# Softmax over rows of 1024: ACT's code aligned to slot 100 of a block of 128 instructions, and 25 buffers in place of 4 for the small tiles

## The chip, the core and the metric

The kernel runs on one core of a Trainium2 chip. A core has engines that run their own instruction streams and wait for one another through semaphores. Four of them matter here: VectorE (DVE in the profile), ScalarE (ACT), GpSimd (POOL) and SyncE (SP). Data moves between the memory of the device (HBM) and the core's own memory (SBUF) by DMA; a transfer is issued from the queue of an engine (here SP, POOL and ACT) and carried out in packets by 16 DMA engines that all queues share.

The metric is the device time of one execution in microseconds (us). Lower is better. Beside the plain runs there is one profiled execution, from which all views of the profile come.

## The reference

```python
def setup_inputs():
    batch, seq, dim = 32, 512, 1024
    return {
        "x": np.random.randn(batch, seq, dim).astype(np.float32),
        "temperature": 0.5,
    }

def reference(x: np.ndarray, temperature: float) -> np.ndarray:
    scaled = x / temperature
    shifted = scaled - np.max(scaled, axis=-1, keepdims=True)
    exp_x = np.exp(shifted)
    return (exp_x / np.sum(exp_x, axis=-1, keepdims=True)).astype(np.float32)
```

That is a softmax over the last axis of 16,384 rows of 1024 float32 numbers: 67.11 MB are read and 67.11 MB are written.

## The kernel before

The 16,384 rows are cut into 11 passes (`PASSES`, line 10). A pass takes 128 partitions times k rows for each partition: 11 rows in the first pass, 12 in each of the nine that follow, 9 in the last. The tile of a pass is one buffer of the pool `data`, which has 4 (line 43); so pass i + 4 can be loaded only when pass i has been stored. A pass is worked on in groups, of 4, 4 and 3 rows in the first, of 6 and 6 in the next nine, and of 4, 3 and 2 in the last. There are 24 groups.

Each group goes through four steps:

- `maximum` (lines 65 to 74): DVE takes the maximum of each row (line 71, into the small tile `top`) and multiplies it by the negative scale (line 74, into `bias`). Each group takes four new small tiles here, `top`, `bias`, `sums` and `recip`, from the pool `stats`, which has 4 buffers for each name (line 44).
- `exponential` (lines 76 to 87): ACT computes the exponential of each row in place and leaves the row's sum in `sums`. Each row is one call on line 80, and two instructions on ACT: ACTIVATE, and ACTIVATION_READ_ACCUMULATOR, which writes the sum. All groups together have 128 such pairs.
- `divide` (lines 89 to 100): DVE takes the reciprocal of the sums (line 92) and multiplies the rows by it: in one instruction for the whole group in passes 2, 3, 4 and 6 (line 95), row by row in the others (line 98).
- `store` (lines 102 to 111): after the last group of a pass the whole tile is stored by one DMA, from POOL's queue in passes 0 to 5 and from ACT's queue in passes 6 to 10 (line 110). Then `load` issues the next load from SP's queue (line 62). Ahead of the first store, POOL copies one element of tile 2 (line 108), so that this store waits until tile 2 has landed.

The order of the work on each engine is the order of the program (`manual_schedule`, line 115). In the steady part, DVE does the maximum of group g + 1 between the maximum and the division of group g, while ACT works on a group's exponentials. From pass 9 on a pass begins only when the groups before it are finished (`ALONE`); the three groups of the last pass have all their maxima and exponentials ahead of the first division (`HELD`).

A buffer of a pool is used again by a later tile of the same name, and the framework puts in the waits for that. With 4 buffers for each small tile, group g writes `sums` where group g - 4 wrote it. On ACT this shows as a wait for a count that ACT itself has set, beside the wait for the group's `bias`. An instruction carries one wait of its own; further waits stand ahead of it as separate instructions (EVENT_SEMAPHORE). The built program of ACT has 300 instruction slots: 256 for the pairs of line 80, 5 stores, one table load, 31 EVENT_SEMAPHORE, and 7 others at its begin and end. DVE's program has 178, SP's 41, POOL's 33. An instruction has 64 bytes.

Of the kernel before, what the change touches and what calls it, by code (L numbers as in the profile page):

```python
# [1 line left out]

# [4 lines left out]

PASSES = [[4, 4, 3]] + [[6, 6]] * 9 + [[4, 3, 2]]  # L10
BUFS = 4

WHOLE = (2, 3, 4, 6)


BY_POOL = 6

ALONE = 9

HELD = len(PASSES) - 1  # L20


@with_exitstack
def kernel(
    ctx: ExitStack,
    tc: tile.TileContext,
    x: bass.AP,
    temperature: bass.AP,
    out: bass.AP,
):  # L30
    nc = tc.nc
    f32 = mybir.dt.float32
    scale = 1.0 / float(temperature)
    extreme = mybir.AluOpType.max if scale > 0 else mybir.AluOpType.min

    P = 128
    xf = x.flatten_outer_dims()
    of = out.flatten_outer_dims()
    n, d = xf.shape
    rows = [sum(ks) for ks in PASSES]  # L40
    assert sum(rows) * P == n

    data = ctx.enter_context(tc.tile_pool(name="data", bufs=BUFS))
    stats = ctx.enter_context(tc.tile_pool(name="stats", bufs=4))


    groups = []
    for i, ks in enumerate(PASSES):
        for j, k in enumerate(ks):
            groups.append((i, sum(ks[:j]), k))  # L50

    def dram(t, i):
        block = t[P * sum(rows[:i]) : P * sum(rows[: i + 1]), :]
        return block.rearrange("(p k) d -> p k d", p=P, k=rows[i])

    tiles, small = [], []

    def load():
        i = len(tiles)
        if i < len(PASSES):  # L60
            xt = data.tile([P, rows[i], d], f32, name="xt")
            nc.sync.dma_start(out=xt, in_=dram(xf, i))  # L62
            tiles.append(xt)

    def maximum(g):
        i, a, k = groups[g]
        top, bias, sums, recip = (
            stats.tile([P, k], f32, name=name) for name in ("top", "bias", "sums", "recip")
        )
        small.append((bias, sums, recip))  # L70
        nc.vector.tensor_reduce(  # L71
            out=top, in_=tiles[i][:, a : a + k, :], axis=mybir.AxisListType.X, op=extreme
        )
        nc.vector.tensor_scalar_mul(bias, in0=top, scalar1=-scale)  # L74

    def exponential(g):
        i, a, k = groups[g]
        bias, sums, _ = small[g]
        for b in range(k):
            nc.scalar.activation(  # L80
                tiles[i][:, a + b, :],
                tiles[i][:, a + b, :],
                mybir.ActivationFunctionType.Exp,
                bias=bias[:, b : b + 1],
                scale=scale,
                accum_out=sums[:, b : b + 1],
            )

    def divide(g):
        i, a, k = groups[g]  # L90
        _, sums, recip = small[g]
        nc.vector.reciprocal(recip, sums)  # L92
        if i in WHOLE:
            xt = tiles[i][:, a : a + k, :]
            nc.vector.tensor_mul(xt, xt, recip.unsqueeze(2).to_broadcast([P, k, d]))  # L95
            return
        for b in range(k):
            nc.vector.tensor_scalar_mul(  # L98
                tiles[i][:, a + b, :], in0=tiles[i][:, a + b, :], scalar1=recip[:, b : b + 1]
            )  # L100

    def store(g):
        i, a, k = groups[g]
        if a + k == rows[i]:
            if i == 0:


                nc.gpsimd.tensor_copy(stats.tile([P, 1], f32, name="seen"), tiles[2][:, 0, 0:1])  # L108
            queue = nc.gpsimd if i < BY_POOL else nc.scalar
            queue.dma_start(out=dram(of, i), in_=tiles[i])  # L110
            load()

    with tc.manual_schedule():
        for _ in range(BUFS):
            load()
        waiting = []

        def finish():  # L120
            for g in waiting:
                divide(g)
                store(g)
            waiting.clear()

        for g, (i, a, k) in enumerate(groups):
            if i >= ALONE and a == 0:
                finish()
            maximum(g)
            exponential(g)  # L130
            if i < HELD:
                finish()
            waiting.append(g)
        finish()


# [1 line left out]
_INS = ['x', 'temperature']  # L138
_OUTS = [((32, 512, 1024), 'float32')]

_NUMBERS = {'temperature': 0.5}


# [26 lines left out]
```

## Time and profile before

| what | us |
|---|---|
| median of 3 runs | 317.6 |
| lowest and highest of the runs | 316.92, 318.63 |
| the profiled execution, its time | 318.96 |
| the profiled execution, its span | 317.2 |
| DVE busy in the span | 252.3 |
| ACT busy in the span | 148.3 |
| POOL busy in the span | 3.7 |

The span reaches from the first to the last instruction of the program; the time of the profiled execution also holds what lies around it, 1.76 us. Busy time leaves out the instructions that only wait or issue a DMA. The DMA part of the profile lists its queues: q1 is what SP issues (the loads), q0 what POOL issues and q10 what ACT issues (the stores), q14 carries the engines' own instructions. A view by windows gives, for each stretch of the span, the busy time of each engine and the mean busy share of the 16 DMA engines.

### The profile page before, as it was taken

How to read it: one execution, taken by the hardware profiler on the slowest of the kernel's cores; microseconds unless marked ns; L12 is line 12 of the kernel's file. 1: busy time of each engine (PE TensorE's matmuls, PEld its weight loads, DVE VectorE, ACT ScalarE, POOL GpSimd, SP SyncE). 2: the span in 40 equal slices, each digit the busy share in tenths (PEclk: the TensorE clock that was granted, in tenths of full speed). 3: DMA queues.
4: the chain of work that ended last, by engine and by line, in shares of the span. 5: the costliest groups of instructions: out<-in, count | busy, mean ns of one | idle time of the engine just before them, and what ended most of it. 6: DMA issues, size and time to landing. Idle time of an engine off the chain costs nothing. (4 is left out here: it accounts for less than half of the span.)

```text
span 317.2 us, 542 instructions
## 1 busy us (share of the span) xinstructions
DVE 252.3 (80%) x160; ACT 148.3 (47%) x257; POOL 3.7 (1%) x11
## 2 busy tenths in 40 slices
DVE  0099999999999799969949994997199689779900
ACT  0048477468174353807171770438035805916600
POOL 0000010000000000000000000000000000000000
DMA  9999999999999999999999999999999999999994
GB/s 364 401 459 397 459 434 377 417 439 438 440 403 465 428 409 471 410 440 440 403 471 415 415 477 397 446 441 409 465 421 409 471 418 431 442 414 459 421 432 181
DMA packets 3171, 134.24 MB, mean 423 GB/s; under 512 B 352, under 2 KB 352, under 8 KB 352
## 3 DMA queue, kind: packets, MB, share of 16 engines
q1 hardware_dynamic: 1584, 67.11, 49.5%
q0 software_dynamic: 864, 37.22, 27.1%
q10 hardware_dynamic: 720, 29.88, 21.8%
q14 instruction: 3, 0.02, 0.0%
HBM read 67.11 MB, written 67.11 MB: 423 GB/s over the span
## 5 line engine op out<-in xcount | busy, mean ns | idle before, releaser
L80 ACT ACTIVATE xt<-xt,bias 128x1024 f32<-128x1024 f32 x128 | 145.2, 1135 | 133.7 <-DVE bias L74 64.6
L71 DVE TENSOR_REDUCE top<-xt 128x6 f32<-128x6144 f32 (+3 forms) x24 | 140.1, 5837 | 40.7 <-DMA xt<-in_x_dram 40.7
L98 DVE TENSOR_SCALAR xt<-xt,recip 128x1024 f32<-128x1024 f32 x80 | 54.5, 748 | 0.6
L95 DVE TENSOR_TENSOR xt<-xt,recip 128x6144 f32<-128x6144 f32 x8 | 52.5, 6559 | 0.6 <-DVE recip L92 0.2
L80 ACT ACTIVATION_READ_ACCUMULATOR xt<-xt,bias 128x1 f32 x128 | 23.8, 186 | 0.0
L80 ACT ACT_TABLE_LOAD x1 | 1.3, 1283 | 16.7 <-DMA xt<-in_x_dram 16.7
L92 DVE RECIPROCAL recip<-sums 128x6 f32<-128x6 f32 (+3 forms) x24 | 4.3, 180 | 5.8 <-ACT xt L80 5.8
L110 POOL DMA_DIRECT2D out_dram<-xt x6 | 3.3, 554 | 129.0 <-ACT xt L80 83.8
L74 DVE TENSOR_SCALAR bias<-top 128x6 f32<-128x6 f32 (+3 forms) x24 | 4.1, 171 | 0.8
L108 POOL COPY seen<-xt 128x1 f32<-128x1 f32 x1 | 0.2, 183 | 45.3 <-DMA xt<-in_x_dram 45.3
L151 POOL MEMSET const-bfloat16-1.0<- 128x1 bf16 x1 | 0.1, 102 | 0.0
L151 POOL MEMSET const-uint8-127<- 128x1 uint8 x1 | 0.1, 102 | 0.0
L151 POOL MEMSET const-float32-0.0<- 128x1 f32 x1 | 0.1, 99 | 0.2 <-issue 0.2
L151 POOL MEMSET const-float32-1.0<- 128x1 f32 x1 | 0.1, 99 | 0.0
## 6 DMA issues: line engine op xcount, KB each, us to landing
xt<-in_x_dram SPq DMA_DIRECT2D x9, 6144.0 KB, 37.1
out_dram<-xt POOLq DMA_DIRECT2D x5, 6144.0 KB, 36.7
out_dram<-xt ACTq DMA_DIRECT2D x4, 6144.0 KB, 32.6
xt<-in_x_dram SPq DMA_DIRECT2D x1, 5632.0 KB, 15.8
out_dram<-xt POOLq DMA_DIRECT2D x1, 5632.0 KB, 28.5
xt<-in_x_dram SPq DMA_DIRECT2D x1, 4608.0 KB, 39.5
out_dram<-xt ACTq DMA_DIRECT2D x1, 4608.0 KB, 15.5
```

What stands on the lines that cost most here:

```text
L71: nc.vector.tensor_reduce(out=top, in_=tiles[i][:, a : a + k, :], axis=mybir.AxisListType.X, op=extreme)
L74: nc.vector.tensor_scalar_mul(bias, in0=top, scalar1=-scale)
L80: nc.scalar.activation(tiles[i][:, a + b, :], tiles[i][:, a + b, :], mybir.ActivationFunctionType.Exp, bias=bias[:, b : b + 1], scale=scal ...
L92: nc.vector.reciprocal(recip, sums)
L95: nc.vector.tensor_mul(xt, xt, recip.unsqueeze(2).to_broadcast([P, k, d]))
L98: nc.vector.tensor_scalar_mul(tiles[i][:, a + b, :], in0=tiles[i][:, a + b, :], scalar1=recip[:, b : b + 1])
L108: nc.gpsimd.tensor_copy(stats.tile([P, 1], f32, name="seen"), tiles[2][:, 0, 0:1])
L110: queue.dma_start(out=dram(of, i), in_=tiles[i])
L151: nc = _bacc.Bacc("TRN2", target_bir_lowering=False, num_devices=1)
```

## The change

Two lines differ. The pool of the small tiles gets 25 buffers for each name; there are 24 groups, so no small tile is used twice. And a directive for ACT's instruction stream stands ahead of the first load: what follows it on ACT is placed at slot 100 of a block of 128 instructions, and (`max_nops=0`) the slots that are left out are passed by a branch and not by instructions that do nothing.

```diff
@@ -41,7 +41,7 @@
     assert sum(rows) * P == n
 
     data = ctx.enter_context(tc.tile_pool(name="data", bufs=BUFS))
-    stats = ctx.enter_context(tc.tile_pool(name="stats", bufs=4))
+    stats = ctx.enter_context(tc.tile_pool(name="stats", bufs=25))
 
 
     groups = []
@@ -113,6 +113,7 @@
 
 
     with tc.manual_schedule():
+        nc.scalar.addr_align(128, offset=100, max_nops=0)
         for _ in range(BUFS):
             load()
         waiting = []
```

In the built program the order of the computing instructions and of the DMAs is the same on every engine, and DVE, POOL and SP have as many slots as before. ACT's program has 287 slots in place of 300: one for the directive is added, and 14 of its 31 EVENT_SEMAPHORE are gone, those that stood for a wait on ACT's own earlier work.

## The prediction

> **What bounds the kernel now.** I read the page's span and DMA rows first, then the windows, then the chain of waits, then the timeline around single ACT instructions, and last the packet records behind the DMA rows (each packet's start, duration and queue).
>
> ```profile
> span 317.2 us, 542 instructions
> DVE 252.3 (80%) x160; ACT 148.3 (47%) x257; POOL 3.7 (1%) x11
> ...
> q14 instruction: 3, 0.02, 0.0%
> HBM read 67.11 MB, written 67.11 MB: 423 GB/s over the span
> ```
>
> No engine is full: DVE idles 65 us, ACT 169 us. The windows (engine busy times, then PEclk, the DMA engines' busy share and GB/s in the last three columns) show what is:
>
> ```profile
> 50.00:100.00 50.00, 49.58 (x30) 28.27 (x49) 1.06 (x2) 1.00 1.00 430
> ...
> 150.00:200.00 50.00, 40.45 (x24) 21.92 (x39) 1.06 (x2) 1.00 1.00 432
> ...
> 250.00:300.00 50.00, 42.44 (x44) 26.93 (x48) 0.00 (x0) 1.00 0.99 428
> 300.00:313.00 13.00, 0.73 (x2) 0.00 (x0) 0.00 (x0) 1.00 0.97 419
> 313.00:317.20 4.20, 0.00 (x0) 0.00 (x0) 0.00 (x0) 1.00 0.06 26
> ```
>
> The 16 DMA engines are busy from 2 us to 313 us with no hole, and move about 430 GB/s whether DVE is at 49.58 or at 40.45 of 50 us. The packet records say it more sharply: of the packets of 49,152 bytes, the median on each of the three data queues is 1.815 us. All packet times together are 312.1 us for each engine. The first data packet starts at 1.76 us, so with equal engines the last would end at about 313.9. In fact most engines end between 312.9 and 313.5, two at 313.9 and 314.4, and one, the straggler, at 315.96 (packets put in line, each starting where one ended). The end of the span waits for that one. It is late because single packets of its own took longer (0.30 us at 99.7, 0.36 at 134.8, 0.46 at 196.8, 0.72 at 242.7), while ACT did nothing special.
>
> ```profile
> DMA 24%; DVE 5%; DVEq 0%; issue 0%; SPq 0%
> ```
>
> The chain of waits agrees: ACT is not on it. So a change pays only if it shortens DMA work, closes the straggler's 2 us, or opens a hole in the DMA engines' work.
>
> **Part 1: 25 buffers.** In the built ACT program 14 EVENT_SEMAPHORE go away. Their waits were for ACT's own earlier sums, four groups back, always long done. What they cost is read where a group starts, as the distance from the end of `bias` to the first ACTIVATE:
>
> ```profile
> 41.70 0.17 DVE L74 TENSOR_SCALAR bias<-top 128x6 f32<-128x6 f32 x1
> ...
> 41.91 1.15 ACT L80 ACTIVATE xt<-xt,bias 128x1024 f32<-128x1024 f32 x1 [6.02 <-DVE bias L74]
> ...
> 50.56 0.17 DVE L74 TENSOR_SCALAR bias<-top 128x6 f32<-128x6 f32 x1
> ...
> 50.83 1.15 ACT L80 ACTIVATE xt<-xt,bias 128x1024 f32<-128x1024 f32 x1 [2.02 <-DVE recip L92]
> ```
>
> Without the extra wait: 41.91 - 41.87 = 0.04 us. With it: 50.83 - 50.73 = 0.10. At 61.76, with two instructions ahead of it, 61.76 - 61.59 = 0.17. So one costs 0.06 to 0.07 us, and 14 cost 0.9 us of ACT's time. I put the gain on the end at 0, and the work that hides it is twofold: DVE divides and takes the next maximum while ACT works (10.9 to 13.4 us a group against ACT's 6.8), and the DMA engines are full whatever DVE does. With all cover gone it would be -0.9 us. The tail has its own cover: the last store is issued at 300.76, its first packet starts at 302.45, and the store before it still has packets until 303.76. An earlier last store only lengthens that queue. No wait is added on any engine, and DVE, POOL and SP issue as before. The other end of the bound is 0: nothing becomes later by a wait that is missing.
>
> **Part 2: the alignment.** What it moves is the moment at which ACT's sequencer crosses from one block into the next. The before trace shows this as the three q14 packets, of 8192 bytes, or 128 instructions of 64 bytes, at 68.73, 134.47 and 208.26 us. To tell whose they are I count slots. At 61.76 ACT's sequencer runs ahead through its own slots 57 to 69 and blocks there; at 202.28 it runs through 191 to 204. These hold places 128 apart (63 to 69 and 191 to 197), so the first and third packets are ACT's, 6.0 to 7.0 us after the crossing (68.73 - 61.76; 208.26 - 202.28). The second is DVE's by the same count (its slots 64 to 67 at 127.8 to 128.3). So 59 to 65 slots lie ahead of ACT's own.
>
> Is ACT held up there? No:
>
> ```profile
> 68.48 0.19 ACT L80 ACTIVATION_READ_ACCUMULATOR xt<-xt,bias 128x1 f32 x1
> 72.55 1.15 ACT L80 ACTIVATE xt<-xt,bias 128x1024 f32<-128x1024 f32 x1 [3.88 <-DVE recip L92]
> ```
>
> ACT starts at 72.55, 0.10 after its `bias` (72.28 + 0.17). In the other crossing, ACTIVATEs of slots 197 to 201 start at 205.68 to 207.95, ahead of the packet at 208.26, so the block being entered was already there and the packet brings a later one. The price on ACT is 0.
>
> After the change, the instruction behind the directive, own slot 6, sits at slot 100. Slot 128 is then own slot 34, in the group of 41.9 us; slot 256 is own slot 162, in the group of 173.3 us. With the delay of 6.0 to 7.0 us I expect ACT's packets near 48 to 49 and near 179 to 180 us, DVE's still near 134. A price if ACT did stall: up to 7 us in such a group. The cover there is the time in which ACT waits for DVE afterwards: 2.02 us before 50.83 and, in the group after, 4.04; near 173 it is 3.97. Also ACT's result is wanted by DVE only at 61.5, after ACT is done at 48.8. DMA has the four loads in line until 70.8, and store 0 from 48 us. So even a stall of 7 us ends before DVE asks.
>
> The price on the DMA engines: a code packet takes 0.31 us, and the data packet next to it 0.11, 0.36 and 0.15 us longer, so 0.42 to 0.67 us on one engine of 16. Two stay two, on engines that end 2.1 and 2.5 us before the straggler. Price 0, unless a packet falls on the straggler; then 0.42 to 0.67 each, 1.3 at most for two.
>
> The branch over some 30 slots is not in the trace; it lies between 0 and the 16.60 us that ACT waits for the first load anyway. I take 0. The Trainium skill ("Runtime: NRT & Kernel Launch", section "Instruction fetch mechanics") speaks against such a branch: a taken branch out of the two loaded blocks has to fetch its target first. By that rule ACT would lose one fetch at its start, and the sum would still be 0, under the 16.60 us of waiting. The same section gives a block as 256 instructions; the trace's packets of 8192 bytes say 128, and that decides.
>
> Sum: 0 + 0 + 0 against the profiled span of 317.2 us (318.96 with the 1.76 around it). That execution lies 1.4 us above the median of the runs, so I forecast the median again: **317.6 us**.
>
> **The rivals.**
>
> *Faster: the straggler evens out.* If moving ACT's two packets lets the late engine keep up with the others, the last packet ends at 313.4 in place of 315.96: 2.5 us off the profiled execution. It would give 318.96 - 2.5 = 316.4 if the plain runs are shorter because they straggle less, and 317.6 - 2.5 = 315.1 if they straggle as much; I take 315.8. For it: the straggler's excess really decides the end. Against it: its long packets (99.7, 196.8, 242.7) are nowhere near ACT's fetches, and the one at 134.8 is next to DVE's fetch, which stays.
>
> *Slower: a third crossing at the end.* ACT's own slots now end at slot 380; before they ended near 360. A few slots after its last instruction ACT enters the block at slot 384, while it goes through the closing steps, where the other engines wait for it. If that block isn't there, it costs at least a packet with its start-up: 0.31 + 1.69 (issue to first packet of the last store, 302.45 - 300.76) = 2.0 us, or with a fetch delayed as under load, 7.0. That gives 319.6 to 324.6; I take 319.6, as the DMA engines are idle by then. It decides if the block wasn't brought by the fetch at slot 256, and if the crossing comes after 310 us, since ACT has nothing to do between 301.1 and 316.6. For it: before, no fourth packet is seen. Against it: each crossing seen so far found its block there.
>
> *The directive does nothing.* If it is dropped, only the 14 instructions are gone, ACT's first crossing stays near 62 us, the second comes some 13 slots later in the program, and the time is 317.6 as well.
>
> **How the numbers follow.** No change (the forecast and the dropped directive) 0.70, of which the dropped directive 0.05; the straggler evened out 0.14; the late crossing 0.16. About 0.5%, 1.6 us, is what a measurement of this kernel can tell from no change: the three runs span 1.7 us. So faster means under 316.0, slower over 319.2. The range is 315.9 to 319.6: from just inside the evened straggler to the late crossing at its lower price.
>
> **What would show it.** Right: q14 packets near 48 and 180 us and one near 134, ACT with no gap that DVE doesn't explain, 0.04 us from `bias` to ACTIVATE in nearly all groups, the DMA share at 1.00 from 17 to 300 us, and 1.815 us for a packet. Wrong: a hole in the DMA rows, a gap in ACT in mid-group, packets that got shorter or longer throughout, or a time outside the span far from 1.76 us.

## The result, and the profile after

The changed kernel takes 319.49 us in the median of 9 runs (318.02 to 319.67), the kernel before 317.24 in 9 runs on the same chip. The ratio is 1.0059, with a 95% interval of 1.0041 to 1.0077: slower, by some 2 us.

The two profiled spans, 317.2 and 317.4 us, do not show this difference. The profiled execution of before (318.96 us) was one of the few long ones of its kernel, so its span is no fair partner. The spans of all timed executions are: of the kernel before 315.0 to 317.3, median 315.5 (30 executions of a later comparison), of the changed kernel 316.0 to 317.8, median 317.6. What lies outside the span went from 1.77 us to 1.95 in the mean. So of the difference of the medians about 2.1 us lie inside the span and 0.18 outside.

The page of the changed kernel, its first lines and the code packets:

```profile
span 317.4 us, 529 instructions
DVE 252.3 (79%) x160; ACT 148.3 (47%) x257; POOL 3.7 (1%) x11
...
q14 instruction: 3, 0.02, 0.0%
HBM read 67.11 MB, written 67.11 MB: 423 GB/s over the span
```

Every engine does the same work in the same busy time; 13 instructions fewer are ACT's. The windows of the changed kernel (the last two columns are the DMA engines' busy share and GB/s):

```profile
50.00:100.00 50.00, 49.58 (x30) 28.30 (x49) 1.06 (x2) 1.00 1.02 430
...
150.00:200.00 50.00, 39.76 (x24) 21.21 (x38) 1.06 (x2) 1.00 1.00 435
...
300.00:313.00 13.00, 0.98 (x2) 0.00 (x0) 0.00 (x0) 1.00 0.98 422
313.00:317.40 4.40, 0.00 (x0) 0.00 (x0) 0.00 (x0) 1.00 0.04 17
```

The DMA engines are still full until 300 us, 0.98 busy from there to 313, and move as much as before. What comes after 313 us is for the most part one engine: in the packet records, half of the 16 engines have ended at 313.3 us and the last one ends at 316.2. To see what that costs, here are the last instructions of an execution without such an engine. It is the kernel before with one harmless copy added (e10 below); the timeline's columns are start, duration, engine, line and operation:

```profile
295.64 1.42 DVE L98 TENSOR_SCALAR xt<-xt,recip 128x1024 f32<-128x1024 f32 x2
297.08 0.34 ACTq L112 DMA_DIRECT2D out_dram<-xt  x1
```

And the same two lines of the changed kernel:

```profile
299.56 1.42 DVE L98 TENSOR_SCALAR xt<-xt,recip 128x1024 f32<-128x1024 f32 x2
301.01 0.34 ACTq L110 DMA_DIRECT2D out_dram<-xt  x1
```

The last store is issued 3.9 us later, because the last load lands later: it took 40.2 us from issue to landing, against 36.1 there. The load has landed only when the slowest of the 16 engines has done its part: in the packet records they end that load between 278.6 and 283.6 us in the changed kernel, between 278.6 and 279.5 in e10. In e10 the last store's engines end between 313.1 and 314.0 us, and the span is 315.2.

The line that the prediction missed is in the view of line 110, ACT's stores, of the kernel before (count, then shortest, median and longest time of an issue, in ns):

```profile
L110 ACTq DMA_DIRECT2D out_dram<-xt x5: 338/338/853, 209.0 to 300.8; - x5
```

The same line of the changed kernel:

```profile
L110 ACTq DMA_DIRECT2D out_dram<-xt x5: 338/338/377, 209.0 to 301.0; - x5
```

The longest issue is the first, the store of pass 6. Before the change it took 853 ns at 208.96 us, right behind ACT's second code packet (208.26 to 208.57), which the window from 208 to 209 us has:

```profile
q14 instruction: 1, 0.01, 1.9%
```

After the change that code packet comes at 179.96, and the issue takes 377 ns. That the issue is delayed next to a code packet is called the hold from here on. The experiments ask what it was worth.

### The profile page after: what moved, and what is told of

Same layout as the page of the kernel before. It is cut to its first block, busy times and chain, and to the rows that moved or that the text cites. A ratio compares the mean times of both kernels' runs of the same rounds, so it can differ in the third digit from the quotient of the medians.

```text
span 317.4 us, 529 instructions
## 1 busy us (share of the span) xinstructions
DVE 252.3 (79%) x160; ACT 148.3 (47%) x257; POOL 3.7 (1%) x11
## 6 DMA issues: line engine op xcount, KB each, us to landing
xt<-in_x_dram SPq DMA_DIRECT2D x1, 4608.0 KB, 40.2
```

## The experiments

Ratios are against the kernel before, run beside each experiment on the same chip, with 95% intervals. They are not quotients of the medians: for e9, a ratio of 1.0022 stands beside medians of 318.75 and 317.21 us. "Span" is the median of the spans of all timed executions, 12 of most kernels. e0 to e7 ran on one chip, e8 to e11, f1 to f4 and g1 and g2 on one other each; the spans of the kernel before on these four are 315.4 to 315.7.

### Which of the two parts it is: e0 to e3

e0 is the kernel before, unchanged.

> The kernel before, unchanged, for a second profile and its own time. All theories: ratio 1.000 (0.997 to 1.003), time near 317.2 us. Theory A (the 2 us lie in the closing steps, where ACT crosses slot 384 a few slots after its own last): time outside the span 1.7 to 1.8 us, no code packet behind the span. Theory B (the 2 us lie inside the span, one DMA engine ends later): in an execution of about 317.2 us the latest DMA engine of the last store ends at about 314.2, 1.5 to 2 us earlier than the 315.96 of the first profile, which was a slow sample at 318.96 us.

Measured: 1.0015 (0.9996 to 1.0034), span 315.55, 1.77 outside. Its profiled execution had a span of 318.2, with the last engine ending at 316.97 and the others at 313.6 to 314.0; the part of theory B about its last engine could not be seen here and was seen in e10. In this execution ACT's second code packet came at 206.17 us and had ended 2.5 us ahead of the store of pass 6, and the issue was not held:

```profile
L110 ACTq DMA_DIRECT2D out_dram<-xt x5: 338/338/376, 209.0 to 301.8; - x5
```

So the kernel before does not always have the hold, and this execution without it was one of its long ones.

e1 has the buffers alone, e2 the alignment alone:

```diff
-    stats = ctx.enter_context(tc.tile_pool(name="stats", bufs=4))
+    stats = ctx.enter_context(tc.tile_pool(name="stats", bufs=25))
```

> 25 buffers, no alignment. Theories A and B (the alignment costs): as before, ratio 0.998 to 1.002, code packets of ACT near 73 and near 215 us (13 slots later). Theory C (the missing waits or the new places of the small tiles cost): ratio 1.005 to 1.008.

> Alignment to slot 100, 4 buffers. ACT's own code then ends at slot 394, so that slot 384 is crossed inside the program, near its last exponentials. Theory A: the late crossing is away from the closing steps, time outside the span 1.7 to 1.8 us, ratio near 1.000. Theory B: code packets near 36, 173 and one near 290 to 305 us, ratio 1.005 to 1.010, the latest engine 2 us or more behind the others. Theory C: ratio 1.000.

Measured: e1 1.0002 (0.9987 to 1.0017), span 315.5, code packets of ACT at 69.0 and 209.5 us. e2 1.0049 (1.0030 to 1.0068), of 6 executions, span 317.15, 1.77 us outside, code packets of ACT at 37.9, 162.9 and 297.5. The alignment costs, the buffers don't. Theory C falls, and so does theory A as an account of the whole: e2 has nothing more outside and is slow.

e3 is the changed kernel with another slot:

```diff
-        nc.scalar.addr_align(128, offset=100, max_nops=0)
+        nc.scalar.addr_align(128, offset=80, max_nops=0)
```

> As the changed kernel with slot 80 in place of 100: ACT's own code ends at slot 360, as before the change, and its code packets fall near 57 and 209 us. Theory A: ratio near 1.000, no code packet just behind the span. Theory B: depends on when the packets fall; if packets in the first 50 us are what hurts, ratio near 1.000 and the latest engine within 1.5 us of the others. Theory C: ratio 1.005 to 1.008.

Measured: 1.0039 (1.0023 to 1.0055), span 317.0, 1.78 outside, code packets of ACT at 47.0 and 188.5 us. The 0.18 us outside are seen with slot 100 and 25 buffers only. In the changed kernel one code packet starts 1.78 us behind the span's end, as this window from 319 to 320 us shows (it has no other packet):

```profile
DMA packets 1, 0.01 MB, mean 8 GB/s; under 512 B 0, under 2 KB 0, under 8 KB 0
...
q14 instruction: 1, 0.01, 3.3%
```

In no profile with another slot or with 4 buffers does such a packet stand behind the span, and all of those kernels have 1.76 to 1.78 us outside. That this packet costs the 0.18 us is likely and not shown: f2 below, with slot 100 and 25 buffers too, has 1.84 us outside and no such packet in its profile.

### The packets' own cost, or their moment: e4 to e7

e4 and e5 are the changed kernel with slots 64 and 40. e6 and e7 are the kernel before with one more load of 8 KB, whose data nothing uses, on ACT's queue behind group 2 or 13 (counted from 0). The edit of e6, without the line that makes the tile `extra`:

```diff
             exponential(g)
+            if g == 2:
+                nc.scalar.dma_start(out=extra, in_=xf[0:2, :].rearrange("(o r) d -> o (r d)", o=1))
```

> The directive with slot 64, which puts ACT's crossings where they were before the change (code packets near 67 and 208 us in the span). Theory B (what hurts is when ACT's code packets fall): ratio 1.000 (0.998 to 1.002). Theory D (the directive itself, its branch or its padding, hurts, wherever it puts the code): ratio 1.004 to 1.006, as with slots 80 and 100.

> The directive with slot 40: ACT's code packets later than before, near 92 and near 225 us. Theory B in its early form (a packet before 50 us, while only loads run, hurts): ratio 1.000. Theory B in its late form (what matters is that the second packet stays near 208 us, ahead of the first store from ACT's queue): ratio 1.004 or more. Theory D: 1.004 to 1.006.

> The kernel before, with one more load of 8 KB from ACT's queue behind the third group, near 36 us, where the changed kernel has its first code packet; its own code packets stay near 68 and 208 us. The 8 KB are read and not used. Early form of theory B: one DMA engine (or as many as share the 8 KB) falls behind by 0.3 to 0.6 us at 36 us, and the end moves by 1 to 2 us: ratio 1.003 to 1.006. Theory D and the late form: 1.000 to 1.001.

> The same 8 KB load behind the 14th group, near 150 us, in the stretch where loads and stores run together. Early form of theory B: 1.000 to 1.002, an engine 0.4 us later at most. Theory that any extra packet on one engine costs the same wherever it falls: the same ratio as with the load at 36 us.

Measured: e4 1.0010 (0.9989 to 1.0030), span 316.25, ACT's packets at 65.6 and 214.1 us. e5 1.0010 (0.9991 to 1.0029), span 316.05, packets at 77.4 and 231.9. e6 1.0030 (1.0010 to 1.0051), span 316.6. e7 1.0034 (1.0015 to 1.0053), span 317.0; its extra load came at 173 us in fact. So the directive as such is not what costs (theory D falls), the late form of theory B falls with e5, and the early moment isn't needed either: 8 KB at 173 us do as much as at 36. In all four the issue of ACT's first store took 0.37 to 0.38 us. In e1 it had been held longest of all:

```profile
L110 ACTq DMA_DIRECT2D out_dram<-xt x5: 338/339/2403, 208.7 to 298.2; - x5
```

This gave theory G, which at this point was a guess: the first store from ACT's queue comes while POOL's last store and a load are under way, so that three queues share the engines; when it comes too early, the engines fall out of step. It does not account for all: e4 and e5 have no hold either, and their spans are only 0.85 and 0.65 us above the kernel before's, where e3's is 1.5 above.

### The hold, put back by hand: e8 to e11, f1 to f4, g1, g2

e8 (changed kernel) and e10 (kernel before) were to hold the store of pass 6 by a copy on POOL; e9 and e11 likewise with 6 rows:

```diff
+            if i == BY_POOL:
+                nc.gpsimd.tensor_copy(tiles[i][:, 0:2, :], tiles[i][:, 0:2, :])
             queue = nc.gpsimd if i < BY_POOL else nc.scalar
```

> The changed kernel, with a copy by POOL of 2 rows of tile 6 onto themselves ahead of the store of pass 6, the first from ACT's queue. It changes no data and makes that store be issued some 1 to 3 us later. Theory G (before the change ACT's second code packet, near 208 us, holds up that first store's issue, and the later issue is what kept the time low; the alignment moves the packet away and the store comes early): the span falls back by 1 us or more, ratio 0.998 to 1.002. Theory B (the moment of the code packets alone, through the packets' own cost on one DMA engine): ratio stays at 1.004 to 1.006.

> The same with 6 rows, so that the store is issued some 4 to 8 us later. Theory G: ratio 0.996 to 1.002, lower than with 2 rows if the overlap of three queues is what costs. Theory B: 1.004 to 1.006. If the delay goes so far that the DMA engines run dry of stores: over 1.006.

> The kernel before with the same copy of 2 rows. Theory G: ratio 0.996 to 1.000, with few or no executions above 318.5 us, since the later issue no longer depends on where the code packet falls. Theory B: 1.000.

> The kernel before with the copy of 6 rows. Theory G: as with 2 rows or lower. Theory B: 1.000.

These failed as a test. The rows were those of the pass's first group, divided some 18 us before the store; the copy ran at 190 us and held nothing (the store was issued 0.11 us after DVE's last instruction). Measured: e8 1.0038 (1.0021 to 1.0054), span 316.7; e9 1.0022 (1.0003 to 1.0041), span 316.85; e10 0.9996 (0.9977 to 1.0014), span 315.3; e11 0.9990 (0.9975 to 1.0004), span 315.4. They serve as controls for the copy itself: e8 and e9 stand 0.75 and 0.9 us of span below the changed kernel, although their copy held nothing. And the two profiles of the kernel before, with spans of 315.2 and 315.1 us, show ACT's first store held by the code packet, as in e1. This is e10's:

```profile
L112 ACTq DMA_DIRECT2D out_dram<-xt x5: 338/338/1752, 208.1 to 297.1; - x5
```

f1 (changed kernel), f3 (e6) and f4 (kernel before) copy rows 6 and 7, of the last group, so that the store has to wait; f2 copies rows 6 to 11 in the changed kernel:

```diff
+                nc.gpsimd.tensor_copy(tiles[i][:, 6:8, :], tiles[i][:, 6:8, :])
```

> The changed kernel; POOL copies 2 rows of the last group of tile 6 onto themselves (1.89 us for such a copy in the profile of e8) ahead of ACT's first store, so that this store is issued about 2 us later. Theory G (the held store kept the kernel before tidy): span median near 315.5 and no long packets at 227 to 270 us; with the 0.18 us more outside the span a ratio of 0.999 to 1.002. Theory B (the early code packets themselves): span 316.7 to 317.6, ratio 1.004 to 1.006.

> The same with 6 rows, about 5.4 us. Theory G: span 315.2 to 315.7 as well, unless the delay leaves the engines without stores. Theory B: 316.7 to 317.6.

> The kernel before with the 8 KB load at 36 us (ratio 1.003 without the delay, its first store not held) and the 2 us of delay. Theory G: ratio 0.999 to 1.001, since the 8 KB cost nothing to speak of. Theory that a small packet on some engines costs 1 us: 1.003.

> The kernel before with the 2 us of delay. Theory G: ratio 0.997 to 1.000, and no execution over 317.9 us, where the kernel before has 3 in 30 to 5 in 35 of them. Theory B: 1.000 with the same share of slow ones.

The timeline of f1 shows that the store now waits for the copy (DVE's division ended at 208.94):

```profile
209.15 1.89 POOL L110 COPY xt<-xt 128x2048 f32<-128x2048 f32 x1 [31.21 <-issue]
211.07 0.38 ACTq L112 DMA_DIRECT2D out_dram<-xt  x1
```

Measured: f1 1.0010 (0.9994 to 1.0025), span 315.8, where the changed kernel had 317.6 and its controls e8 and e9 316.7 and 316.85. By ratio, f1's interval lies below the changed kernel's and overlaps with those of both controls. f2 1.0030 (1.0018 to 1.0042), span 316.4, of 5 executions: more delay is not better. f3 1.0004 (0.9988 to 1.0021), span 316.1 against 316.6 for e6. f4 1.0007 (0.9995 to 1.0018), span 315.35; two of its 12 executions were still over 317.9 us (6 of 29 of the kernel before beside it), so theory G's promise that there would be none was not kept.

g1 is e5 with the copy of rows 6 and 7, g2 is e3 with it.

> Slot 40, 25 buffers (ratio 1.001, span 316.05 without the delay, code packets of ACT at 77 and 232 us) with ACT's first store held by POOL's copy of 2 rows. Theory G: span 315.1 to 315.5, ratio 0.997 to 1.000; if a version beats the kernel before it is this one, as its second code packet also lies behind the stretch in question. Theory that the hold only matters together with early code packets: span stays at 316.

> Slot 80, 25 buffers (ratio 1.0039, span 317.0 without the delay, code packets of ACT at 47 and 188 us) with the same delay. Theory G: span 315.4 to 315.9, ratio 1.000 to 1.001.

Measured: g1 1.0002 (0.9984 to 1.0021), span 315.75 against 316.05 for e5. g2 1.0002 (0.9987 to 1.0017), span 315.75 against 317.0 for e3, whose interval lies wholly above. A copy that holds nothing was not tried with slot 80. No version beats the kernel before.

What the hold does to the DMA engines is in the packet records. Each row is one profiled execution: how far apart the 16 engines end the load of pass 7 (their drift at about 194 us, before ACT's first store), when the issue of that store ended, the starts of the first and the sixteenth of its packets, how far apart the engines end the load of pass 8 (about 225 us), by how much packets from 220 to 300 us are longer than usual for their size, in sum, and the ends of the last store on the median and on the last engine. All are us.

| profile | load 7 | issue ended | first packets | load 8 | longer by | median, last engine | span |
|---|---|---|---|---|---|---|---|
| before | 1.7 | 209.82 | 213.5 to 216.5 | 4.0 | 0.89 | 313.3, 316.0 | 317.2 |
| e0, before, not held | 1.7 | 209.34 | 213.8 to 216.1 | 4.4 | 1.63 | 313.7, 317.0 | 318.2 |
| after | 1.5 | 209.38 | 213.0 to 216.0 | 3.3 | 1.91 | 313.3, 316.2 | 317.4 |
| e1, 25 buffers, held by the code packet | 1.5 | 211.07 | 214.9 to 217.2 | 2.3 | 0.24 | 313.2, 315.1 | 316.4 |
| e2, slot 100, 4 buffers | 1.9 | 209.57 | 213.3 to 215.9 | 3.7 | 1.91 | 313.4, 316.2 | 317.5 |
| e3, slot 80 | 1.4 | 209.04 | 212.2 to 215.4 | 3.6 | 5.79 | 313.2, 315.9 | 317.2 |
| e5, slot 40 | 0.7 | 208.64 | 211.7 to 215.5 | 2.6 | 1.27 | 313.2, 314.3 | 315.5 |
| e10, before, held by the code packet | 0.7 | 209.90 | 215.2 to 216.0 | 0.9 | 0.32 | 313.4, 314.0 | 315.2 |
| e11, before, held by the code packet | 0.7 | 209.82 | 215.1 to 216.0 | 0.9 | 0.00 | 313.3, 313.9 | 315.1 |
| f1, slot 100, held 2 us | 1.8 | 211.45 | 215.0 to 217.0 | 3.6 | 0.40 | 313.2, 314.9 | 316.1 |
| f2, slot 100, held 5 us | 1.2 | 214.55 | 217.7 to 219.2 | 3.2 | 2.64 | 313.4, 315.2 | 316.4 |
| f4, before, held 2 us | 0.8 | 210.44 | 214.9 to 216.0 | 1.1 | 0.39 | 313.3, 314.0 | 315.2 |
| g2, slot 80, held 2 us | 1.2 | 210.93 | 214.9 to 216.3 | 1.4 | 0.37 | 313.3, 314.3 | 315.5 |

Two things go together. Where the first store's packets begin near 215 us, they begin on all engines within 0.9 to 2.3 us, and few packets are long afterwards. Where they begin at 211.6 to 213.8, the engines take the store up 2 to 4 us apart; single packets near 227 us (of the store), 242 and 270 us (of loads) then take 0.1 to 0.9 us longer than usual, and one or a few engines end late. f2, held for longer, has such packets too. Over all 20 profiles, the nine with first packets from 214.9 us on have spans of 315.1 to 316.4 us, the eleven with earlier ones 315.5 to 318.2.

The hold counts together with how far the engines have drifted by then. With a drift of 0.7 us it makes little difference: the spans are 315.1 to 315.6 with it (e10, e11, f3) and 315.5 without (e5). With 1.2 us they are 315.5 and 316.4 with it (g2, f2), and 317.1 and 317.2 without (e7 and e9). With 1.7 to 1.9 us they are 316.1 with it (f1), and 317.5 and 318.2 without (e2 and e0). The row of before is the caution: its issue ended 0.1 us ahead of e10's and its engines were already 1.7 us apart, and it ended like the unheld ones. Each row is one execution, and not always a usual one: those of e5 and e11 are the fastest of their 12, f1's is the second slowest of 11. What makes the engines drift before 194 us was not tested. Why an engine that is out of step has such long packets the records do not tell.

## Why the prediction was wrong, point by point

**What bounds the kernel** was right: the DMA engines' busy share is 0.91 to 0.96 from 2 to 17 us, 1.00 from 17 to 300 and 0.97 to 0.99 from 300 to 313 in every profile here, the usual packet of 49,152 bytes takes 1.815 us in all of them, and the last engine sets the end (316.2 us and a span of 317.4; 314.0 and 315.2 in e10).

**The straggler was misread.** The prediction took the profiled execution's late engine, 2 us and more behind, as the kernel's habit and as room for a gain. It belongs to the kernel's few long executions (3 of 30 to 8 of 35 are over 317.9 us): the profile said 318.96 us where the runs said 317.6. In e10, e11 and f4 the last engine is 0.6 to 0.7 us behind the median; after the change all 9 executions are over 317.9. The rival "the straggler evens out" had the sign the wrong way round.

**Part 1, 25 buffers at 0**: right, 1.0002. The wait is gone where it was seen. In the changed kernel, `bias` ends at 50.76 and ACT starts at 50.80, 0.04 us later in place of 0.10:

```profile
50.59 0.17 DVE L74 TENSOR_SCALAR bias<-top 128x6 f32<-128x6 f32 x1
```

```profile
50.80 1.15 ACT L80 ACTIVATE xt<-xt,bias 128x1024 f32<-128x1024 f32 x1 [1.96 <-DVE bias L74]
```

**Part 2, "The price on ACT is 0"**: this is the step that failed. The prediction looked for gaps in ACT's computing, found none, and none came: the first ACTIVATE of every group starts within 0.2 us of what it waits for in all 20 profiles. But ACT also issues stores, and the prediction does not weigh these, though line 110's view had 853 ns against 338. In the four profiles where the hold was seen (before, e1, e10, e11) the issue ended 1.22 to 1.25 us after the code packet did; where the store came 1.4 us or more behind the packet's end (e0, f3, f4), its issue took 0.38 us. The alignment took the code packet away from that place, the issue ended 0.4 to 0.5 us earlier (209.38 against 209.82 in before and 209.90 in e10), and by the experiments this cost some 1 us, where the prediction had 0 for ACT and 0 for the DMA engines.

That the lost hold is a cause is supported best by slot 80, 1.0039 without a hold and 1.0002 with it (intervals apart), and in the changed kernel by f1, 1.0010 against 1.0059 (intervals apart). Two things limit this. e3 and g2 were measured on different chips, and so were f1 and its controls, each version beside the kernel before. And the controls e8 and e9, where the copy held nothing, stood at spans of 316.7 and 316.85, already 0.75 to 0.9 us under the changed kernel's 317.6; f1, at 315.8, is 0.9 to 1.05 below them. So about 1 us of the 2.1 in the span is the hold's; whether the other part comes from the copy itself, from the chip or from one comparison to the next is open. f3 and g1 point the same way within their intervals. Nor is it the whole: f1's span is 0.3 us above the kernel before, 0.17 us stay outside, and e4 and e5 lost the hold at less cost. Whether the earlier moment of ACT's code packets (36 to 47 us with slots 100 and 80, 66 to 77 with 64 and 40) adds to it stays open.

The cover for a stall on ACT was misread too. The prediction has DVE want the result of the group of 41.9 us only at 61.5. That is the next group's; this group's division begins with the reciprocal at 50.64, 1.8 us after ACT is done at 48.8:

```profile
50.64 0.18 DVE L92 RECIPROCAL recip<-sums 128x6 f32<-128x6 f32 x1
```

A stall of 7 us would have made DVE wait some 5. As no stall came, this did not matter.

**"Two stay two", the packets' own price on the DMA engines**: the prices were right (a code packet took 0.31 us, its neighbour 0.11 to 0.36 us more), and in the changed kernel both of ACT's packets may lie on the engine that ended last (packets of several engines start together there, so the line is not certain). Yet in e3 and e4, where the line of the last engine can be followed back packet by packet to 2 and to 52 us, it carried no code packet on the way. Their own price isn't what decides there.

**The moments**: 179.96 us for the second packet was within the forecast of 179 to 180, DVE's at 133.7 too; the first came at 36.1, not 48 to 49, one group earlier. So the place in a block from which a fetch goes out was not known as well as the count of slots pretended, and the statement that the block being entered was already there was inferred and has not been shown.

**"A third crossing at the end"**: the place was right, the price far off. The packet is there, 1.78 us behind the span, and 0.18 us go with it where 2.0 was forecast. The measured 319.49 us lies beside this rival's 319.6, and inside the range, by luck: 2.1 of the difference lie inside the span, where this rival has nothing. Slot 80, which ends ACT's code 20 slots earlier, has none of it.

**The branch**: the Trainium skill's rule ("Runtime: NRT & Kernel Launch", "Instruction fetch mechanics") that a taken branch may cost a fetch of its target was priced at 0 under ACT's first wait. With slots 64 and 40 a code packet does appear at 1.76 us, and ACT's first exponential is not late by it (21.22 and 21.36 us, 21.27 before); with slots 80 and 100 none appears there.

**"The directive does nothing"**: false for what it moves; it moved both of ACT's packets by some 30 us.

## What to carry to other kernels

An engine that computes in time may still be late, or early, with its DMA issues: read the shortest, median and longest issue of each queue, and treat an odd one as part of the schedule. Here, with the DMA engines full, an earlier store on a third queue gained nothing: it went with engines that were out of step and with a later end. And compare a profile's own time with the runs before building on one late engine in it: one execution can be the odd one.

## What had not been expected of the hardware

The issue of ACT's first store took 0.37 to 0.38 us alone and 0.85 to 2.40 us where one of ACT's code packets came between 0.9 us after its start and 0.4 us before it. In e6 and e7, where ACT had issued an earlier DMA, the code packet fell at 208.5 and 208.3 us, close to the store's issue at 208.2 and 208.6, and the issue took 0.38 us all the same. Whether the earlier DMA or the few slots that it adds made the difference was not tried.

Moving ACT's instructions to other slots moved the end by 2 us, more than six times what one code packet takes on its DMA engine (0.31 us). One 8 KB load, 0.006% of the data, went with 1.2 to 1.6 us of span.
